# A 2 KB copy from DRAM to DRAM on the queue of ScalarE, beside the first load of a rotary-embedding kernel

## The chip, the cores and the metric

The kernel runs on one core of one Trainium2 chip. The metric is the device time of one execution in microseconds (us). The profile of one execution gives a span that is about 2 us shorter than that time.

## The reference, cut to what matters

```python
# x: (16, 512, 16, 64) float32: batch, seq, heads, dim;  cos, sin: (512, 32)
x1, x2 = x[..., :32], x[..., 32:]
first  = x1[..., :16] * cos[..., :16] - x1[..., 16:] * sin[..., :16]
second = x1[..., :16] * sin[..., :16] + x1[..., 16:] * cos[..., :16]
out = concatenate([first, second, x2], axis=-1)     # x2 passes through untouched
```

Input and output are 33.55 MB each. In DRAM each head of a row is 256 bytes: 128 bytes that are rotated, then 128 bytes that only pass through.

## The kernel before

Four tiles of 8.4 MB go through a ring of three buffers in SBUF. Loads and stores are long rows (16 to 64 KB for each partition), all on SyncE's queue; the untouched half rides along in them. VectorE rotates the first half of each head in place. The GpSimd queue loads the small cos and sin tables.

```python
def load(t, lo=0, hi=K):
    nc.sync.dma_start(out=rows(t, lo, hi), in_=xf[t, :, lo * R : hi * R])
def store(t, lo=0, hi=K):
    nc.sync.dma_start(out=of[t, :, lo * R : hi * R], in_=rows(t, lo, hi))
# ... cos and sin loaded on the GpSimd queue ...
load(0, 0, K0)          # a quarter of tile 0, 2 MB
load(0, K0, K)          # the rest of it
load(1)
load(2, 0, KC)          # first half of tile 2
# ... tables built on VectorE ...
rotate(0, 0, K0); rotate(0, K0, (K0 + K) // 2); rotate(0, (K0 + K) // 2, K)
store(0)
load(2, KC, K)          # second half of tile 2
load(3)                 # its ring buffer is tile 0's: waits until store(0) has landed
for t in range(1, T):
    rotate(t, 0, KC); rotate(t, KC, K)
    store(t)
```

## Time and profile before

| | before |
|---|---|
| time, median of the first 3 runs | 162.67 us (162.45 to 162.75) |
| span of the profiled run | 160.9 us |
| bytes moved by DMA | 67.24 MB |
| VectorE busy | 112.9 us, 70% |
| DMA engines without a packet, per engine, up to the last packet at 159.56 us | 2.26 us: 1.90 at the start, 0.32 at the end |

The last row is worked out from the packet records in the trace: at each moment, the share of the 16 DMA engines that have no packet. (A record does not name its engine; where this text speaks of one engine, records were strung together, each to the one that starts as it ends.) The page of the profile says the same more roughly. From part 2 (busy tenths in 40 slices of the span; a long packet is counted in the slice in which it starts, so the digits swing between 6 and 9) and part 3 (queue: packets, MB, share of 16 engines' span):

```profile
DMA  6999999969999996999996996998998998998992
...
q1 hardware_dynamic: 1440, 67.11, 97.7%
q0 software_dynamic: 64, 0.13, 0.2%
```

SyncE's queue alone keeps all 16 engines busy for 97.7% of the span. In the packet records a load or store piece of 65,536 bytes takes 2,418 ns at the median, which is 27.1 GB/s per engine, and the next one starts as it ends. So the kernel is bound by bytes through the DMA engines.

The chain of waits, however, also names VectorE (start in us, length in us, what):

```profile
43.37 29.64 DMA out_dram<-ring
73.02 0.02 issue
73.03 28.86 DMA ring<-in_x_dram
101.89 0.03 issue
101.92 0.02 DVEq L98
101.94 0.04 issue
101.99 4.45 DVE b_t L98
```

It reads: store(0) is issued at 43.37 us and lands 29.6 us later; only then is the load of tile 3 issued, which lands at 101.9 us; VectorE then rotates tile 3, and the last store is issued at about 129 us. This chain is not what bounds the kernel as it stands, because the engines always have older transfers queued meanwhile.

### The profile page before, as it was taken

To read this page: it belongs to the slowest core of one execution; us is meant where nothing else is said; L and a number is where in the kernel's file an instruction comes from. 1 tells how busy PE (TensorE), PEld (TensorE's weight loads), DVE (VectorE), ACT (ScalarE), POOL (GpSimd) and SP (SyncE) were. 2 spreads that over 40 slices of the span, in tenths; PEclk is the share of its full clock that TensorE was granted. 3 is DMA by queue.
4 is the path that set the end of the run, shared out by engine and by line. 5 is a ranking of instruction groups with operands and counts; after the bars stand their busy time and mean duration, and the time that the engine had idled before them with its cause. 6 is when DMAs were issued, how large, how long until landed. Compare 5 with 4: busy or idle time off the path is not lost.

```text
span 160.9 us, 116 instructions
## 1 busy us (share of the span) xinstructions
DVE 112.9 (70%) x47; POOL 1.4 (1%) x6
## 2 busy tenths in 40 slices
DVE  1049999999999999999999991699999900000000
POOL 3000000000000000000000000000000000000000
DMA  6999999969999996999996996998998998998992
GB/s 195 554 391 391 391 456 521 521 261 521 391 391 261 521 521 261 521 391 391 472 570 261 521 521 261 521 423 358 521 423 358 521 423 358 521 423 358 521 423 98
DMA packets 1504, 67.24 MB, mean 418 GB/s; under 512 B 192, under 2 KB 192, under 8 KB 224
## 3 DMA queue, kind: packets, MB, share of 16 engines
q1 hardware_dynamic: 1440, 67.11, 97.7%
q0 software_dynamic: 64, 0.13, 0.2%
HBM read 33.69 MB, written 33.55 MB: 418 GB/s over the span
## 4 chain that ended last, share of the span: by engine, by line
DMA 50%; DVE 28%; DVEq 1%; issue 0%; SPq 0%
DMA ring<-in_x_dram 31%; DMA out_dram<-ring 18%; DVE b_t L98 10%; DVE ring L99 10%; DVE ring L100 5%; DVE ring L103 3%; DVEq L142 1%; SPq L55 0%; DVEq L98 0%
## 5 line engine op out<-in xcount | busy, mean ns | idle before, releaser
L98 DVE TENSOR_TENSOR b_t<-ring,table 128x4096 f32<-128x4096 f32 (+2 forms) x9 | 35.6, 3959 | 5.4 <-DMA ring<-in_x_dram 5.2
L99 DVE TENSOR_TENSOR ring<-ring,table 128x4096 f32<-128x4096 f32 (+2 forms) x9 | 35.6, 3950 | 0.3
L100 DVE TENSOR_TENSOR ring<-ring,b_t 128x2048 f32<-128x2048 f32 (+2 forms) x9 | 18.4, 2049 | 0.3
L103 DVE TENSOR_TENSOR ring<-ring,b_t 128x2048 f32<-128x2048 f32 (+2 forms) x9 | 18.4, 2042 | 0.0
L74 DVE LOAD_MASK_SELECT spun<-stage x1 | 0.0, 14 | 8.7 <-DMA stage<-in_sin_dram 8.7
L84 DVE COPY table<-packed 32x1024 f32<-32x1024 f32 x4 | 2.7, 684 | 0.1
L81 DVE COPY packed<-spun 32x512 f32<-32x512 f32 (+3 forms) x4 | 1.7, 416 | 0.1
L61 DVE MEMSET stage<- 128x512 f32 x1 | 0.5, 485 | 0.9 <-PEq L131 0.9
L74 DVE STREAM_SHUFFLE spun<-stage 128x512 f32<-128x512 f32 x1 | 0.7, 722 | 0.0
L63 POOL DMA_DIRECT2D stage<-in_cos_dram x1 | 0.6, 649 | 1.3 <-DVE stage L61 1.3
L64 POOL DMA_DIRECT2D stage<-in_sin_dram x1 | 0.5, 532 | 0.0
L131 POOL MEMSET const-bfloat16-1.0<- 128x1 bf16 x1 | 0.1, 96 | 0.0
L131 POOL MEMSET const-float32-0.0<- 128x1 f32 x1 | 0.1, 93 | 0.2 <-issue 0.2
L131 POOL MEMSET const-float32-1.0<- 128x1 f32 x1 | 0.1, 93 | 0.0
L131 POOL MEMSET const-uint8-127<- 128x1 uint8 x1 | 0.1, 93 | 0.0
## 6 DMA issues: line engine op xcount, KB each, us to landing
ring<-in_x_dram SPq DMA_DIRECT2D x2, 4096.0 KB, 44.9
ring<-in_x_dram SPq DMA_DIRECT2D x1, 6144.0 KB, 21.6
ring<-in_x_dram SPq DMA_DIRECT2D x1, 2048.0 KB, 7.7
stage<-in_cos_dram POOLq DMA_DIRECT2D x1, 64.0 KB, 6.3
stage<-in_sin_dram POOLq DMA_DIRECT2D x1, 64.0 KB, 7.7
out_dram<-ring SPq DMA_DIRECT2D x4, 37.2
ring<-in_x_dram SPq DMA_DIRECT2D x2, 34.7
```

Source lines behind the costliest of these rows:

```text
L61: nc.vector.memset(stage[:, :, :, 0:Q], 0.0)
L63: nc.gpsimd.dma_start(out=spread[:, 0, 0], in_=cosf)
L64: nc.gpsimd.dma_start(out=spread[:, 0, 1], in_=sinf)
L74: nc.vector.stream_shuffle(out=spun[:], in_=stage.rearrange("p t k j -> p (t k) j")[:, :, 0:Q], mask=[j % PQ * REP for j in range(PB)],)
L81: nc.vector.tensor_copy(out=packed[0:n], in_=spun[q * PB : q * PB + n])
L84: nc.vector.tensor_copy(out=table[r * PB : (r + 1) * PB].rearrange("p t k c j -> p (t k) c j"), in_=packed.unsqueeze(2).to_broadcast((PB, ...
L98: nc.vector.tensor_mul(out=b_t, in0=x1, in1=s)
L99: nc.vector.tensor_mul(out=x1, in0=x1, in1=c)
L100: nc.vector.tensor_sub(out=x1[:, :, :, 0:Q], in0=x1[:, :, :, 0:Q], in1=b_t[:, :, :, Q:HF])
L103: nc.vector.tensor_add(out=x1[:, :, :, Q:HF], in0=x1[:, :, :, Q:HF], in1=b_t[:, :, :, 0:Q])
L131: nc = _bacc.Bacc("TRN2", target_bir_lowering=False, num_devices=1)
L142: with _tile.TileContext(nc) as tc:
```

## The change

The diff adds one small transfer on a queue that nothing used. For 16 rows (the first of every batch), it copies the untouched 128 bytes of head 0 straight from input to output, with no pass through SBUF. The stores still write the same bytes later, so nothing is saved; the change asks what a DRAM-to-DRAM transfer on a second queue costs beside a full first queue.

```diff
     load(0, 0, K0)
+
+    step = B * S // 16
+    xr = x.rearrange("b s h d -> (b s) (h d)")
+    outr = out.rearrange("b s h d -> (b s) (h d)")
+    nc.scalar.dma_start(
+        out=outr.rearrange("(e r) n -> e r n", r=step)[:, 0, HF:D],
+        in_=xr.rearrange("(e r) n -> e r n", r=step)[:, 0, HF:D],
+    )
     load(0, K0, K)
```

## The prediction

> **What bounds the kernel now.** The 16 DMA engines, by bytes. The page's queue table gives SyncE's queue 67.11 MB and 97.7% of 16 engines' span of 160.9 us. In the trace's packet records a 65,536-byte packet takes 2,418 ns at the median (27.1 GB/s per engine, loads and stores alike), and from 2.3 us, when the last engine has its first packet, to 158.9 us, when the first runs out, no engine idles by any amount worth counting. The Trainium skill ("DMA: Bandwidth & Descriptors", Specifications) gives about 27 GiB/s per engine; the trace is a little below that. VectorE, 70% busy, is not the limit: its last idle stretch (4.9 us before 102.0 us) waits for the last tile's load, itself queued behind other transfers. When it hands over the last store at 129 us, the engines have some 11 us of older stores queued (estimate: 25.2 MB left at 101.9 us, at 16 x 27.1 GB/s). The issuing side has slack; each nanosecond of engine time goes into the span one for one.
>
> **What the change does.** It removes nothing: the stores still write all 33.55 MB and overwrite the 16 pieces with the same values. It adds one transfer, 16 rows x 128 bytes, on ScalarE's queue, unused before. Sixteen rows should give one piece per engine plus one 4-byte semaphore write. It adds an issue on ScalarE (SyncE's take 0.4 to 0.5 us) and probably a wait of the stores for the small transfer, as both write the output; the first store is issued at 43.4 us, long after.
>
> **Cost.** The Trainium skill (same page, Issuing engines are not separate DMA queues) says that transfers of different issuers "run on the same 16 DMA engines and interleave with each other". The trace agrees where GpSimd's table loads pass among the load packets: a 4,096-byte packet takes 159 ns, a semaphore write 9 ns, and the other queue goes on right behind. Per engine:
> - a 128-byte packet, 10 to 160 ns (estimate from those two), plus 9 ns: about 0.1 us
> - two things may add. If ScalarE's issue comes before SyncE's first load (0.74 us), the whole stream starts up to 0.4 us later. And first packets took 0.9 to 1.5 us where later ones of that size take 0.61; if DRAM to DRAM exposes such a latency, that is at most 0.7 us more. I expect most of this to hide under the load's own start, and take 0.1 us.
> - one more semaphore in the final wait: hundredths.
>
> All of it lies on the critical path, but sums to about 0.2 us, 0.1%.
>
> **Prediction.** 162.9 us, 8 in 10 between 162.5 and 163.8. Chances: faster by over 2% 0.01, within 2% 0.96, slower by over 2% 0.03.
>
> **What would show it.** Queue table: one more hardware queue with 32 packets (16 of 128 bytes, 16 of 4), about 0.0% of the engines; SyncE's queue unchanged. Issue table: the small transfer lands 2 to 6 us after issue. Chain of waits: the same members (loads, VectorE on tiles 0 and 3, the final store), each within some tenths of a us. The first load's landing and all later ones shift by the same 0.1 to 0.4 us.
>
> **What would make it wrong.** One 128-byte piece holding its engine for 2 us or more. The piece split by element instead of by row (512 packets of 4 bytes). A second active queue slowing the packets of the first (65,536 bytes in clearly more than 2,418 ns). Stores waiting for something later than the small transfer, so that the engines run dry.

## The result, and the profile after

Ratios here and below are the mean time of one kernel's fast runs over the mean of the other's of the same rounds, so they are not quite the ratio of the medians quoted. Differences in us, where nothing else is said, are of the two medians of the same rounds.

| | before | after |
|---|---|---|
| time, median of 4 runs each | 162.6 us (162.45 to 162.75) | 162.77 us (162.39 to 163.08) |
| ratio | | 1.0009, 95% interval 0.9985 to 1.0033 |
| span of the profiled run | 160.9 us | 160.6 us |
| DMA engines without a packet, per engine, up to the last packet | 2.26 us | 2.28 us |
| from the last packet to the end of the span | 1.39 us | 1.43 us |

The page of the changed kernel, same lines as before (q10 is the new queue, that of ScalarE):

```profile
DMA  6999999969899996999996996996996997997991
...
q1 hardware_dynamic: 1440, 67.11, 97.7%
q0 software_dynamic: 64, 0.13, 0.2%
q10 hardware_dynamic: 32, 0.00, 0.0%
```

The second queue has 32 packets, and SyncE's queue is unchanged to the packet. The timeline shows ScalarE's issue in the same instant as SyncE's first (start, length, engine, line, operation), and the page's issue table shows when it landed (KB each, us from issue to landing):

```profile
0.74 1.88 SPq L55 DMA_DIRECT2D ring<-in_x_dram  x4
0.74 0.58 ACTq L70 DMA_DIRECT2D out_dram<-in_x_dram  x1
```

```profile
out_dram<-in_x_dram ACTq DMA_DIRECT2D x1, 2.0 KB, 6.2
```

The copy lands at 0.74 + 6.2 = 6.9 us. The packet records tell what it did to the engines. These are consecutive records of the trace across several of the 16 engines (start in us, queue, bytes, ns):

```
5.362  q10    128 bytes   13 ns
5.372  q1   16384 bytes  611 ns
5.374  q10    128 bytes   13 ns
5.383  q1   16384 bytes  611 ns
5.435  q10    128 bytes   13 ns
5.444  q1   16384 bytes  611 ns
```

Each engine has moved five load pieces by then and slips in one 128-byte piece. Its next piece, a load piece or one of the table loads, starts 9 to 10 ns after the start of the small one (once 18). All 16 pieces took 13 ns and their 16 semaphore writes 9 ns each. Between 4 and 7 us all but three of the 75 load pieces keep their 611 ns (two are longer, 773 and 881 ns; the kernel before has two such, 651 and 741), and the median of the 65,536-byte pieces is 2,418 ns as before.

The chain of waits, the lines that answer to those above:

```profile
43.42 29.32 DMA out_dram<-ring
72.75 0.02 issue
72.77 28.83 DMA ring<-in_x_dram
101.59 0.03 issue
101.62 0.02 DVEq L106
101.64 0.04 issue
101.69 4.45 DVE b_t L106
```

The same members in the same order. Store(0) is issued 0.05 us later and the last tile's load lands 0.3 us earlier; shifts of this size, with both signs, cannot be told from the spread between single executions.

The last row of the table is a difference that does repeat. From the last packet to the end of the span pass 1.38 to 1.39 us in the two kernels without a copy (before, and load_early below), and 1.43 to 1.47 us in all eleven that have one (one profiled execution each). So the copy adds about 0.05 us at the end of the program. That its semaphore in the final wait is the reason is likely, but not shown.

### The profile page after: what moved, and what is told of

It is laid out like the page before. It is cut to its first block, busy times and chain, and to the rows that moved or that the text cites. A ratio compares the mean times of both kernels' runs of the same rounds, so it can differ in the third digit from the quotient of the medians.

```text
span 160.6 us, 118 instructions
## 1 busy us (share of the span) xinstructions
DVE 112.9 (70%) x47; POOL 1.4 (1%) x6
## 4 chain that ended last, share of the span: by engine, by line
DMA 50%; DVE 28%; DVEq 1%; issue 0%; SPq 0%
DMA ring<-in_x_dram 31%; DMA out_dram<-ring 18%; DVE b_t L106 10%; DVE ring L107 10%; DVE ring L108 5%; DVE ring L111 3%; DVEq L150 1%; SPq L55 0%; DVEq L106 0%
```

## The experiments

Theory A, from the prediction: the copy costs its engines what its pieces take, 13 + 9 ns each; its latency (the time from issue to landing), its issue and the stores' wait for it are all real but hidden, because of where it stands. Its rivals: B, a copy so small costs nothing anywhere; C, it costs some tenths of a us that four runs could not show. Eleven kernels were run; all give the correct result. Each is compared with the kernel before on the same chip in the same rounds.

| run | what it is | median us | before, same rounds | ratio (95% interval) |
|---|---|---|---|---|
| after_again | the changed kernel | 162.76 | 162.62 | 1.0005 (0.9988 to 1.0022) |
| sp_first | copy on SyncE, ahead of the first load | 163.63 | 162.62 | 1.0060 (1.0046 to 1.0073) |
| sp_behind | copy on SyncE, behind the first four loads | 171.62 | 162.62 | 1.0549 (1.0532 to 1.0567) |
| last | copy on ScalarE, after the last store | 165.00 | 162.62 | 1.0141 (1.0123 to 1.0159) |
| load_early | no copy; one load ahead of store(0) | 171.96 | 162.77 | 1.0559 (1.0541 to 1.0577) |
| behind_kept | sp_behind, queue order kept | 165.34 | 162.77 | 1.0148 (1.0129 to 1.0167) |
| all_rows | copy of 8,192 rows, 128-byte pieces | 171.06 | 162.77 | 1.0501 (1.0481 to 1.0521) |
| wide | the same bytes in 64 KB pieces, 2 MB apart | 166.64 | 162.77 | 1.0234 (1.0204 to 1.0265) |
| wide_near | 64 KB pieces side by side | 165.06 | 162.71 | 1.0145 (1.0128 to 1.0162) |
| two_heads | all_rows with two heads | 178.27 | 162.71 | 1.0956 (1.0925 to 1.0986) |
| whole_head | all_rows with 256-byte pieces | 172.39 | 162.71 | 1.0593 (1.0573 to 1.0614) |

### The changed kernel again

No edit; more rounds.

> The changed kernel once more, with more rounds. Theory A (the 16 pieces cost their engines 13 + 9 ns each, all else of the copy is hidden under the loads): ratio to before 1.000 to 1.002. Rival C (the copy costs some tenths of a us, the first four runs were too few to show it): ratio 1.003 or more, interval clear of 1.

The ratio is 1.0005 and its interval reaches from 0.9988 to 1.0022, that is from 0.2 us less to 0.4 us more. The 0.022 us per engine that the trace shows, and the 0.05 us at the end, lie within it and cannot be told from zero by timing. Rival C, as stated, falls: 1.003 is outside. A cost of up to about 0.36 us is not excluded by timing; against it stand only the packet records.

### The same copy, ahead of the first load

```diff
+    nc.sync.dma_start(out=..., in_=...)      # the 2 KB copy
     load(0, 0, K0)
-    nc.scalar.dma_start(out=..., in_=...)
```

> The same 2 KB copy, issued by SyncE ahead of its first load. Theory A: the copy's own engine time is still nothing, but SyncE's issue of 0.4 to 0.6 us now stands before the first load, so the first load packet starts at 2.1 to 2.4 us instead of 1.74 us and the time rises by 0.3 to 0.6 us (ratio 1.002 to 1.004). Rival B (a copy this small costs nothing wherever it stands): first load packet at 1.75 us, ratio 1.000.

It costs 1.0 us (ratio 1.0060). From the timeline and the issue table of this run:

```profile
0.74 0.60 SPq L69 DMA_DIRECT2D out_dram<-in_x_dram  x1
...
1.39 2.26 SPq L55 DMA_DIRECT2D ring<-in_x_dram  x4
```

```profile
out_dram<-in_x_dram SPq DMA_DIRECT2D x1, 2.0 KB, 2.1
```

SyncE is held for 0.60 us by the copy's issue, so the first load is issued at 1.39 us instead of 0.74, and its first packet starts at 2.58 us instead of 1.75. The copy's own pieces took 11 ns. B falls: the same 2 KB are not free here. The size was larger than the 0.3 to 0.6 us expected, in part because the load's first packet came 1.19 us after its issue instead of 1.0; why the second issue is slower to reach the engines is left open. These two account for 0.83 us; the rest is within the spread of single runs. What follows for the change: ahead of the first load an issue on SyncE costs about 1 us, which an issue on ScalarE in the same instant does not. The copy on SyncE just behind the first load, where the change has it on ScalarE, was not run.

The first load pieces after the copy still took 0.75 to 1.32 us instead of 0.61. The slow first pieces that the prediction feared thus belong to the loads; the 128-byte pieces, here the very first on the engines, do not show it.

### The same copy, behind the first loads on SyncE

```diff
     load(2, 0, KC)
+    nc.sync.dma_start(out=..., in_=...)      # the 2 KB copy
```

> The same copy, on SyncE's queue behind the four loads that start the kernel. Theory A: the stores write the same output, so they wait for the copy; its packets come behind all the loads' packets, at about 52.5 us, and it lands at about 54 us, so the first store is issued at about 54 us instead of 43.4 us, after the engines have run dry; they idle for 2 to 3.5 us and the time rises by that (ratio 1.012 to 1.022). Rival B: ratio 1.000, first store at 43.4 us.

It costs 9.0 us, about three times what theory A said. The engines did run dry, but at 139 to 149 us, not at 52 us. The timeline shows why the expectation missed:

```profile
2.68 0.61 SPq L73 DMA_DIRECT2D out_dram<-in_x_dram  x1
3.33 0.57 SPq L55 DMA_DIRECT2D ring<-in_x_dram  x1
52.14 18.51 SPq L58 DMA_DIRECT2D out_dram<-ring  x2
```

The load at 3.33 us is the second half of tile 2. In the source it stands after store(0); the scheduler that orders each engine's queue had moved it ahead. The x2 in the last line is a second move: store(1) follows store(0), ahead of the load of tile 3. So this run changed two things at once: the store's wait for the copy, and the order of the queue. The next two runs take them apart.

### The order alone

```diff
-    store(0)
     load(2, KC, K)
+    store(0)
```

(on the kernel before, with no copy at all)

> The kernel before, without any copy, but with the second half of tile 2 loaded ahead of the first store; that is the order into which the scheduler had put SyncE's queue in sp_behind. Theory D (the order alone cost sp_behind its 9 us: the first store's packets come behind 4.2 MB of load, so the load of tile 3, which waits for that store, and with it the last store come later and the engines run dry at the end): about 171.6 us, ratio 1.05 to 1.06, engines idle at about 140 to 149 us. Rival E (the store's wait for the copy cost it): ratio 1.00.

It takes 171.96 us, as sp_behind took 171.62. Theory D holds: the order of the queue alone costs the 9 us. In the chain of waits:

```profile
43.49 38.57 DMA out_dram<-ring
82.06 0.02 issue
82.07 39.04 DMA ring<-in_x_dram
```

Store(0) is issued at the same 43.5 us, but its packets now stand behind 4.2 MB of load, and it lands 38.6 us after its issue instead of 29.6. The load of tile 3, which needs the buffer, is issued at 82.1 us instead of 73.0, and in its turn stands behind store(1), which is ready at about 70.4 us. So it lands at 121 us instead of 102, and VectorE hands over the last store 19 us later. The edit did not ask for that second part: in the source the load of tile 3 stands before store(1). The scheduler swapped them here too, as the timeline shows, first the kernel before, then this run:

```profile
73.03 0.33 SPq L55 DMA_DIRECT2D ring<-in_x_dram  x1
73.46 55.74 SPq L58 DMA_DIRECT2D out_dram<-ring  x3
```

```profile
43.49 27.24 SPq L58 DMA_DIRECT2D out_dram<-ring  x2
82.07 0.34 SPq L55 DMA_DIRECT2D ring<-in_x_dram  x1
```

The 9 us are thus the price of both moves together; no run has only the first.

Older transfers last until about 139 us only; the windows view of this run shows the rest (stretch, its length, VectorE busy, POOL busy, granted clock, DMA share, GB/s):

```profile
139.00:149.00 10.00, 8.99 (x4) 0.00 (x0) 1.00 0.17 72
```

In the kernel before the same stretch is full:

```profile
139.00:149.00 10.00, 0.00 (x0) 0.00 (x0) 1.00 0.97 419
```

Summed from the packet records, the engines are without a packet for 9.3 us in this stretch, which is the whole difference.

### The wait alone

sp_behind with every load and store of SyncE pinned behind the one before it in the source:

```diff
-        nc.sync.dma_start(out=rows(t, lo, hi), in_=xf[t, :, lo * R : hi * R])
+        tc.keep_in_program_order(
+            nc.sync.dma_start(out=rows(t, lo, hi), in_=xf[t, :, lo * R : hi * R])
+        )
```

(and the same in store)

> sp_behind with every load and store of SyncE pinned to the order of the kernel before, so that only the store's wait for the copy is left. Theory A: copy packets at 51 us, landing at about 52.1 us, first store issued then instead of at 43.4 us; the engines have run dry at 51.4 us and see the first store packet about 1 us after its issue, so they idle for 1.5 to 3 us at 51 to 54 us and the time rises by that: 164 to 165.6 us, ratio 1.009 to 1.018. Rival B: ratio 1.000. Rival E: 171 us.

It takes 165.34 us, 2.6 us more, inside the expected 164 to 165.6. The waits of SyncE's queue (for whom: us in total, times, longest) name the copy, and the timeline shows the delayed store:

```profile
SPq L61 <- DMA out_dram<-in_x_dram: 29.2, 1, 29.2
```

```profile
52.29 0.36 SPq L61 DMA_DIRECT2D out_dram<-ring  x1
```

The copy's pieces pass at 51.0 to 51.6 us, behind all load packets. It lands at 52.3 us, and only then is store(0) issued, 8.9 us later than before. But the loads kept the engines busy for most of that; they are without a packet for 1.96 us between 51 and 54 us. Of a delay of 8.9 us on the issuing side, 2 us become idle engines, because the queue in front of the store was about 7 us deep. Of the rest of the 2.6 us, the packet records show 0.3 us per engine in packets that took longer than in the kernel before. Pinning without the copy was not run; SyncE's first four issues stand where they did (0.74 to 2.62 us) and the order is that of the kernel before, so it should add nothing. The run also shows that the stores do wait for the copy. In the changed kernel the same wait costs nothing: the copy landed at 6.9 us, 36 us before the store was ready.

### The same copy, last

```diff
     for t in range(1, T):
         ...
         store(t)
+    nc.scalar.dma_start(out=..., in_=...)    # the 2 KB copy, waits for the stores
```

> The same copy on ScalarE's queue, but after the last store in the program, so that it waits for the stores. Theory A: nothing is left to hide its latency; issue (0.5 us), start of the packets (about 1 us) and landing (about 1 us) are added whole: 2 to 3 us more (ratio 1.012 to 1.019). Rival B: ratio 1.000.

It costs 2.4 us (ratio 1.0141). The timeline and the issue table:

```profile
159.94 0.58 ACTq L121 DMA_DIRECT2D out_dram<-in_x_dram  x1
```

```profile
out_dram<-in_x_dram ACTq DMA_DIRECT2D x1, 2.0 KB, 2.1
```

The issue is at 159.94 us, when the last store has landed. The first 128-byte piece follows at 161.31 us and takes 11 ns; the landing is 2.1 us after the issue, and the span ends at 163.1 us instead of 160.9. So a transfer whose engine time is 0.02 us has a latency of 2.1 us, and here all of it shows. B falls again. The pieces came on engines that had been idle for about 2 us and were no slower for it.

### Many short pieces

```diff
-        out=...[:, 0, HF:D],  in_=...[:, 0, HF:D],
+        out=...[:, :, HF:D],  in_=...[:, :, HF:D],
```

(head 0 of all 8,192 rows, still beside the first load on ScalarE: 512 pieces of 128 bytes for each engine)

> The copy of the changed kernel over all 8192 rows instead of 16: 512 pieces of 128 bytes for each engine, 1.05 MB. Theory A (each piece takes its engine 13 ns, as the 16 did): 512 x 13 ns = 6.7 us more, ratio 1.04. Rival F (bytes count alone, at 27.1 GB/s per engine): 2.4 us more, ratio 1.015. Rival G (a single piece hid a cost of short writes to DRAM that a row of them shows): 15 us or more, ratio above 1.09.

It costs 8.3 us: nearest to A's 6.7, three and a half times what F allows, far from G. The queue table, and the wait of the first store:

```profile
q1 hardware_dynamic: 1440, 67.11, 93.3%
q10 hardware_dynamic: 8208, 1.05, 5.1%
```

```profile
SPq L58 <- DMA out_dram<-in_x_dram: 49.2, 1, 49.2
```

The pieces pass one by one between load packets, 30 on each engine until 51 us, against 30 packets of the loads (27 pieces and 3 semaphore writes) in that time. The other 480 or so follow when the loads are done, one in 9.4 to 11.8 ns on each engine, until 57.1 us. Store(0) waits for them and the engines stand idle for 1.9 us until its first packets. So 6.4 of the 8.3 us are left for engine time (5.9 by the spans of the two profiled runs), near A's 6.7, and 1.9 us are the stall of behind_kept, which the expectation had left out. (The table's 5.1%, 8.6 us for each engine, is more because the records of neighbouring pieces overlap: 12 to 25 ns each, one every 9.4 to 11.8.)

### Twice as many, and twice as long

```diff
-        out=...[:, :, HF:D]        # all_rows
+        out=...[:, :, 0:2, HF:D]   # two_heads: heads 0 and 1, 1,024 pieces of 128 bytes
+        out=...[:, :, 0:D]         # whole_head: 512 pieces of 256 bytes
```

(one line each; the input side is cut alike)

> all_rows with two heads: 1,024 pieces of 128 bytes for each engine. In all_rows the pieces went over the engines at one in 11 ns while nothing else ran (482 pieces of each engine in 5.4 us), and the first store then waited for the copy with the engines idle for 1.9 us. Theory A (time per piece, and one stall of 1.9 us): 512 more pieces add 512 x 11 ns = 5.6 us to all_rows, about 13.9 us above before, ratio 1.085, stall again 1.9 us. If the cost per piece rises with the number, clearly more.

> all_rows with 256-byte pieces (the whole head): 512 pieces of each engine, twice the bytes. If the piece is what costs (theory A): as all_rows, 8 to 9 us above before. If bytes cost (256 bytes against 128 at the same rate): twice the engine time of all_rows, 6 us more than all_rows, 14 us above before. In between: a fixed part and a part by bytes.

The queue table of two_heads, then of whole_head:

```profile
q10 hardware_dynamic: 16400, 2.10, 10.6%
```

```profile
q10 hardware_dynamic: 8208, 2.10, 5.4%
```

Two_heads is 15.6 us above before, where 13.9 were expected: the second 512 pieces cost 7.3 us, 14.2 ns each, instead of 11. The stall is 2.2 us. The rate of the pieces falls from about 106 to about 80 in a us on each engine during the copy (in all_rows to 85), with one us at 57; why is open. Whole_head is 9.7 us above before, with a stall of 1.7 us: 256-byte pieces pass at one in 14.1 ns. So the piece costs something beside its bytes: 128 bytes take 9 to 12 ns, and 256 bytes not twice that but 14 ns. At the 27.1 GB/s of long pieces they would take 4.7 and 9.4 ns; but two things beside the length differ. In these runs the 16 stretches of the copy lie 2 MB apart, which slows even long pieces (next section), and the 128-byte pieces start in the middle of a head. No run separates these, so how much of the time is the price of a short piece stays open.

### The same bytes in long pieces

```diff
-        out=...[:, 0, HF:D]
+        out=...[:, 0:16]                                      # wide: 16 pieces of 64 KB, 2 MB apart
+        out=outr[0:256].rearrange("(e r) n -> e r n", e=16)   # wide_near: side by side
```

(one line each; the input side is cut alike. The copy also moves halves not yet rotated; the stores, which wait for it, overwrite them.)

> The same 1.05 MB as in all_rows, but as 16 contiguous stretches of 64 KB, one for each engine. Theory A and rival F agree: 65,536 bytes at 27.1 GB/s is 2.42 us for each engine, so 2.4 us more, ratio 1.015; all_rows above this shows the cost of short pieces. If DRAM to DRAM is slower than load or store for long pieces too, it is clearly more than 2.4 us.

> wide with its 16 stretches of 64 KB side by side in one megabyte, instead of 2 MB apart. wide took 3.9 us more, not the 2.4 us that its bytes are worth: its 16 packets took 3.2 us each where 2.42 was expected, and load packets beside them slowed too. Theory P (the distance of 2 MB made all 16 engines meet in the same part of the DRAM): packets of 2.4 to 2.6 us, 2.4 to 2.8 us more in all. Theory Q (a long piece from DRAM to DRAM slows its engine and its neighbours wherever it lies): again 3 us or more per packet and 3.6 to 4.2 us more.

The new queue in the queue table, for wide and then for wide_near:

```profile
q10 hardware_dynamic: 32, 1.05, 2.0%
```

```profile
q10 hardware_dynamic: 32, 1.05, 1.5%
```

Wide cost 3.9 us where 2.4 were expected: its 16 pieces took 3.25 us at the mean instead of 2.42. That is not the whole account: table and load pieces beside them took 1.3 us longer in all on each engine, while the load pieces of 32,768 bytes took 1.4 us less (in the kernel before, two on each engine take 1.5 to 2.4 us instead of 1.21, at 48 to 52 us, the last two ahead of the first store's). Wide_near costs 2.35 us (ratio 1.0145), and 15 of its 16 pieces take 2,418 ns, exactly as a load or a store of that size (the other one 2,420). P's forecast holds and Q falls: from DRAM to DRAM is not slower in itself. What differs is where the 16 stretches lie, 2 MB apart or side by side; that they meet in the same part of the DRAM is not shown. The Trainium skill ("DMA: Bandwidth & Descriptors", Latency and other measured facts) has a row on HBM row pitch (the distance from one row to the next): for copies of 128 rows of 16 KiB, 164 GB/s at a pitch of 2 MiB against 214 at full rate, 77%. Here, for 16 rows of 64 KB, the ratio is 2.42 to 3.25, 74%, so this case is near it. The mechanism behind it was not tested. The 16 pieces of the change are also 2 MB apart; whether that costs a piece of 128 bytes anything is not shown, since every run with short pieces has this distance.

## Why the prediction was right

The prediction was 162.9 us, within 2%; measured were 162.77 us and a ratio of 1.0009. Point by point:

- **The bound.** "The 16 DMA engines, by bytes" is right. Wide_near is the cleanest evidence: 1.05 MB more at 27.1 GB/s per engine is 2.42 us, and 2.35 us were measured.
- **"One piece per engine plus one 4-byte semaphore write"** is right: 32 packets.
- **"10 to 160 ns" for a piece, "plus 9 ns: about 0.1 us."** 13 + 9 = 22 ns, so the small end of the range. The term was four to five times too large, and far below what timing can resolve. All_rows tests the same term 512 times over, at 6.4 us of engine time, 12.5 ns a piece.
- **A cold latency exposed by DRAM to DRAM, taken as 0.1 us.** There was none, and not because the engines were already running: the pieces took 13 ns after each engine's fifth load packet, but 11 ns as the very first pieces (sp_first) and after 2 us of idle engines (last). What exists is the time from issue to landing (2.1 us in last), and that was hidden.
- **"One more semaphore in the final wait: hundredths"** fits: about 0.05 us from the last packet to the end of the span, in every run with a copy. Theory A, as the experiments state it, had left it out.
- **"If ScalarE's issue comes before SyncE's first load, the whole stream starts up to 0.4 us later."** In the changed kernel both issue at 0.74 us and the first load packet starts at 1.74 us (1.75 before), so it did not happen. The size was wrong: with the copy truly ahead on SyncE it costs 1.0 us.
- **"Probably a wait of the stores for the small transfer"** is right and harmless here; behind_kept shows the wait, and what it costs when the copy lands late.
- **"Lands 2 to 6 us after issue"**: 6.2 us, just outside: the new queue's first turn came only after five load packets.
- **"The first load's landing and all later ones shifted by the same 0.1 to 0.4 us"** is wrong: no shift can be told from the spread (0.05 us later at 43 us, 0.3 us earlier at 102 us).

So the mechanism was right: the pieces pass between load pieces and all else is hidden. The sum of 0.2 us is not confirmed: the trace supports 0.02 us of engine time and about 0.05 us at the end, under 0.1 us, and a forecast of no cost at all would have fitted the times as well. That the two medians differ by 0.17 us, close to the 0.2, is luck.

## What to carry to other kernels

In this kernel, whose DMA engines are all busy, a small extra transfer costs the engine time of its pieces, and its latency only if something must wait for it: the same 2 KB cost nothing that timing could tell beside the first load on a second queue, 1.0 us ahead of it on the first queue, 2.4 us at the end, and 2.6 us where the first store had to wait for it. Look at when it lands and who waits, rather than at its bytes; and after any edit compare the order of each queue with the source, since a load moved ahead of a store, and the swap that the scheduler added to it, cost 9 us here, more than any copy of 2 KB by itself. As for taking the untouched half past SBUF altogether: at 11 ns for 128 bytes, 16.8 MB are 8,192 pieces on each engine, or about 90 us, where riding along in the loads and then in the stores, in long pieces, takes twice 38.7 us, 77 us (estimates from all_rows and the 27.1 GB/s). And the loads and stores of the other half would then be short pieces too, which no run has tried. No version here beats the kernel before.

## What the Trainium skill lacked or had wrong

- "DMA: Bandwidth & Descriptors" (Queues, rings and completion order) says that an engine drains a whole packet, typically 9 to 17 descriptors, from one queue before it switches. Here the turn was one record of the profile, whatever its size: in all_rows 30 pieces of 128 bytes went against 30 packets of the loads on each engine. So this second queue of short pieces moved very slowly beside a first one of long pieces: 30 of 512 pieces in 46 us.
- The same page (Specifications) gives about 0.6 us to the first byte for SyncE and ScalarE, and does not say from when it counts. Here, on free engines, the copy's first piece came 1.4 us after the start of its issue and 0.8 us after the issue's end (sp_first and last), the first load piece 1.0 and 0.6 us. Beside a full queue the copy's first piece came 4.6 us after the start of its issue, after five load packets on each engine; in all seven runs with a copy at this place it came at 5.3 to 5.4 us. No page has this delay; its cause was not tested.
- The same page (Specifications) gives 512 bytes as the smallest transfer for full rate, with a read-modify-write below. It has no measured rate for short pieces from DRAM to DRAM: here 128 bytes took 9 to 12 ns in a long row of them (at 11 ns, 12 GB/s per engine), and 256 bytes 14 ns (18 GB/s), against 27.1 GB/s for 64 KB side by side and 20 GB/s for 64 KB that lie 2 MB apart, as the short pieces did. Whether a read-modify-write took part is not shown.
